# Low parts of the first stream's weight pieces by an adding DMA, and a softmax scaled negative in the masking operation

## The chip, the cores and the metric

The program runs on one core of a Trainium2 chip. The metric is the device time of one execution in microseconds (us). Before the change it is 1472.54 us, the median of 3 runs (1470.87 to 1472.68). The core has a matrix engine (PE, TensorE; its weight loads are PEld), three engines for vectors (DVE = VectorE, ACT = ScalarE, POOL = GpSimd), SP, which issues most of the DMAs, and 16 DMA engines that all queues share.

## The reference, cut to what matters

Two transformer blocks on 512 tokens of width 1024, in float32. The first block has a projection `proj = hn @ w_in`, then three kinds of attention on it, and a gated feed-forward layer; the second has a latent attention with 8 heads, a gated recurrence and a merge.

```python
def token_mixer(...):
    proj = hn @ w_in                       # q_a, k_a, v_a, q_i, k_i, w_i, q_b, k_b, v_b
    out_a = dsa_attention(...)             # 8 heads, keys chosen by a top-256 of an index score
    out_b = diff_attention(...)            # softmax(q1 k1) - lam * softmax(q2 k2), 4 heads
def first_block / second_block:
    s = where(causal, q @ k.T * scale, -inf); p = softmax(s); o = p @ v
```

The queries of every attention are normalised (rmsnorm) per head, so that the scale of a row of scores differs from token to token.

## The kernel before, in words

Products are formed from two parts of each number: `h`, the number rounded to the short format fp32r that PE multiplies at full rate, and `l`, what the rounding left. `mm3` (L217 to L220) takes three multiplications for each tile: h by h (L218), h by l (L219) and l by h (L220), all of them through PE in the order of its queue.

A weight matrix comes in pieces of 128 x 1024 numbers, 512 KB each. `split` (L167) loads a piece into a raw buffer WR (3 buffers, SP's queue), copies it to WH (4 buffers) with rounding, on ACT (L175) or POOL (L173), and subtracts: WL = WR - WH (L176, 4 buffers), on DVE or POOL. `setw` names who does it: two letters, the first for the copy ("a" ACT, "p" POOL), the second for the subtraction ("d" DVE, "p" POOL). WH and WL hold two chunks of two pieces, so the pieces of chunk c + 2 are made while PE works on chunk c + 1.

The first stream (L746 to L790) is the projection: first `w_in0` (matmuls of 452 columns), then 8 chunks of `w_inc` with 2 pieces each: keys, queries and values of two halves of the differential attention, and two chunks of queries of the chosen-key attention. Their 16 pieces are made in mode "ap". Between the multiplications of a chunk PE transposes what the chunk before has become: the outputs leave PSUM through ACT, are squared and summed per head (`head_ss`, L424; `head_scale`, L574), go through the rotation (`rope_bank`: two products on POOL, L415 and L416, two operations on DVE, L417 and L418) and come back to PE as transposes (`tr`, L437; `trr`, L441). The index score (L800 to L808) and the choice of the 256 best keys (L819, L822, on DVE) run between them. The sum over the squares of the input, `Stats.finish`, is one DVE addition (L285) before a small multiplication on PE (L287), which stands in PE's queue ahead of chunk 0.

The attentions follow, interleaved with later weight pieces of `w_xk` and `w_xv` (also "ap", L857). `soft` (L604) is their softmax: for each tile of scores a DVE operation adds the mask and takes the row's maximum (L609), a second small DVE operation multiplies it by minus the row's scale (L612), and ACT takes exp(scale * x + that) and the row's sum (L617); `recips` (L620) divides.

The order on each engine is fixed when the program is built, by a scheduler with a simulation of its own; each engine then works through its queue in order.

Of the kernel before, what the change touches and what calls it, by code (L numbers as in the profile page):

```python
# [15 lines left out]
OP = mybir.AluOpType  # L16
# [46 lines left out]
def _body(nc, tc, ctx, d):  # L63
# [57 lines left out]
    def f32(ap):  # L121
        return ap.bitcast(F32)
# [44 lines left out]
    def split(src, h, l, raw=None):  # L167
        raw = wr_()[:, :src.shape[-1]] if raw is None else raw
        nc.sync.dma_start(raw, src)
        m = wmode[wturn[0] % len(wmode)]  # L170
        wturn[0] += 1
        if m[0] == "p":
            PTS(h, raw, 1.0, 0.0, op0=OP.mult, op1=OP.add)  # L173
        else:
            ACT(h, raw, AF.Copy)  # L175
        (TT if m[1] == "d" else PTT)(l, raw, f32(h), op=OP.subtract)  # L176

    class W:

# [391 lines left out]
        c_ = slice(nt0 * P, nt0 * P + 256)  # L571
        hilo(dsts[:, 0:2, c_], dsts[:, 2:4, c_], p3)

    def head_scale(ps, nt0, out):  # L574

        s_ = head_ss(ps, 4)
        t = sm(8)
        for nn in range(2):
            TS(t[:, nn * 4:nn * 4 + 4], s_[:, nn * 4:nn * 4 + 4], st0["m64"][:, nt0 + nn:nt0 + nn + 1], None, op0=OP.add)
        if len(out.shape) == 3:  # L580
            PTT(out, t.rearrange("p (n h) -> p n h", n=2), nhalf[:, :8].rearrange("p (n h) -> p n h", n=2), op=OP.pow)
        else:
# [18 lines left out]
    s1r = kp(8)
    s1r = Ring([s1r[:, 2 * i:2 * i + 2] for i in range(4)])

    def soft(srcs, mask, scales, N, dst, su=None):  # L604

        n = len(srcs)
        mx, nb = sm(n), sm(n)
        for i in range(n):
            nc.vector.tensor_tensor_reduce(dst[i], srcs[i], mask, 1.0, LOWEST, op0=OP.add, op1=OP.max,  # L609
                                           accum_out=mx[:, i:i + 1])  # L610

            TS(nb[:, i:i + 1], mx[:, i:i + 1], scales[:, i:i + 1], -1.0, op0=OP.mult, op1=OP.mult)  # L612
        if su is None:
            su = sm(n)
            su = [su[:, i:i + 1] for i in range(n)]
        for i in range(n):
            ACT(dst[i], dst[i], AF.Exp, scale=scales[:, i:i + 1], bias=nb[:, i:i + 1], accum_out=su[i])  # L617
        return su

    def recips(su):  # L620
        ri = sm(len(su))
        for i, a in enumerate(su):
            nc.vector.reciprocal(ri[:, i:i + 1], a)
        return ri

    class Diff:
# [7 lines left out]
        def chunks(self):  # L634
            def k_mid(ps, nt0):
                rs, t = sm(8), sm(8)
                head_scale(ps, nt0, rs)
                TS(t, rs, 8.0, None, op0=OP.mult)
                return rope_bank(ps, 4, nt0, st0["tab_kb"], t)

            def q_mid(ps, nt0):
                head_scale(ps, nt0, self.qs[:, nt0 * 4:nt0 * 4 + 8])
                return rope_bank(ps, 4, nt0, st0["tab_qb"])

            def v_mid(ps, nt0):
# [15 lines left out]
        def pair(self, b, fring, rring, out):  # L661
            hf, kb, qb, vb, qs = self.hf, self.kb, self.qb, self.vb, self.qs
            N = P * (b + 1)
            om = 1.0 - LINIT
            v = {}

            def stage_a(hh):
                if hh == 0:
                    v["s1"] = s1r()
                pss = []  # L670
                for c in range(2):
                    ps = psc()[:, :N]
# [12 lines left out]
                v["a", hh] = sms[0]

            def stage_b(hh):
                a = v["a", hh]
                pt = ptr()
                for j in range(b + 1):  # L690
                    tr(pt[:, j * P:(j + 1) * P], a[:, j * P:(j + 1) * P])
                ph, pl = rring(F32R)[:, :N], rring(F32R)[:, :N]
                hilo(ph, pl, pt[:, :N])
                v["p", hh] = ph, pl

            def stage_c(hh):
                ph, pl = v["p", hh]
                if hh == 0:
                    v["po"] = out()
                po = v["po"]  # L700
                for j in range(b + 1):
                    s_ = slice(j * P, (j + 1) * P)
                    mm3(po[:, hh * P:(hh + 1) * P], ph[:, s_], pl[:, s_], vb[:, j, hh, 0], vb[:, j, hh, 1],
                        j == 0, j == b)

            def stage_d():
                po = v["po"]
# [6 lines left out]
                ACT(q1, v["s1"], AF.Square, scale=math.sqrt(EPS) / om)  # L714
# [148 lines left out]
    def dsa_unit(g, b):  # L863
# [4 lines left out]
        def stage_a():  # L868
            assert b in chosen
            v["s"] = [fD() for _ in range(4)]  # L870
            for q2 in range(2):
                pss = []
                for hh in range(2):
# [6 lines left out]
                su = soft(pss, mask, qas[:, b, g * 4 + q2 * 2:g * 4 + q2 * 2 + 2], N, dst)  # L880
                ri = recips(su)
# [363 lines left out]
    def latent_fin1(kk, nt0):  # L1245
# [83 lines left out]
    class Mla:  # L1329
# [59 lines left out]
        def unit(self, hh, b):  # L1389
# [3 lines left out]
            def stage_a():  # L1393
# [460 lines left out]
```

## Time and profile before

| | |
|---|---|
| runs, median of 3 | 1472.54 us (1470.87 to 1472.68) |
| profiled execution | 1471.03 us |
| its span, first to last instruction | 1469.2 us |
| PE busy | 1427.6 us, 97% |
| DVE busy | 972.4 us, 66% |
| ACT busy | 570.9 us, 39% |
| POOL busy | 500.8 us, 34% |
| mean granted clock of PE | 0.991 of full speed |

A clock of 1.00 is PE's upper level (2.4 GHz), 0.50 the lower (1.2 GHz); a value between them is a mean over a stretch that had both. PE's operations are pipelined, so that the time from one start to the next says more than the duration of one.

### The profile page before, as it was taken

The page shows a single profiled execution, that of the slowest core. Times are in us where ns is not written, and L with a number is a line of the kernel's source. Part 1 is how long each engine was busy: PE and PEld are TensorE (multiplying, and loading weights), DVE is VectorE, ACT ScalarE, POOL GpSimd, SP SyncE. Part 2 cuts the span into 40 slices and gives each one's busy share as a digit, 9 for nine tenths or more (in the row PEclk, how much of TensorE's full clock was granted, in tenths as well). Part 3 has the DMA queues.
Part 4 walks back from the last instruction along what each step waited for, and adds up shares of the span by engine and source line. Part 5 has one row for each costly group of instructions (what it writes and reads, how often), then busy time and mean ns, then how long its engine had stood idle before and what let it go on. Part 6 is the DMA issues. An engine that isn't in the chain of part 4 may idle for free.

```text
span 1469.2 us, 21193 instructions
## 1 busy us (share of the span) xinstructions
PE 1427.6 (97%) x7920; PEld 1237.1 (84%) x7920; DVE 972.4 (66%) x1920; ACT 570.9 (39%) x1148; POOL 500.8 (34%) x455
## 2 busy tenths in 40 slices
PE   6989999999999999999999999999999999999998
PEld 5888889888878788888888988888888898888887
DVE  8899889755445776356665556666548778885553
ACT  4535768844542322112223344444322333342121
POOL 6665666445531332223321111111114324331110
PEclk9999989999999999999999999999999999999999
DMA  6121143234213222332323432223442221257522
GB/s 215 60 72 58 44 144 117 97 97 132 90 44 101 86 89 85 99 115 89 100 76 95 129 105 94 95 95 106 139 130 86 72 100 67 93 165 239 185 65 86
DMA packets 56023, 152.69 MB, mean 104 GB/s; under 512 B 6000, under 2 KB 13680, under 8 KB 55920
## 3 DMA queue, kind: packets, MB, share of 16 engines
q1 hardware_dynamic: 55776, 151.33, 32.4%
q8 instruction: 62, 1.02, 0.3%
q14 instruction: 41, 0.34, 0.1%
q10 hardware_dynamic: 144, 0.00, 0.0%
HBM read 135.58 MB, written 15.73 MB: 103 GB/s over the span
## 4 chain that ended last, share of the span: by engine, by line
PE 81%; DVE 11%; issue 4%; ACT 2%; POOL 1%; DMA 1%; SPq 0%; POOLq 0%; DVEq 0%; ACTq 0%
PE PS L218 19%; PE PS L219 19%; PE PS L220 18%; PE PT L218 7%; PE PT L220 7%; PE PT L219 7%; PE PS L437 2%; DVE S L822 1%; DVE keep L819 1%; DVE R L155 1%; DVE WL L176 1%; PE PS L1400 1%; DVE S L808 0%; PE PS L876 0%; DMA S<-xT_d 0%
## 5 line engine op out<-in xcount | busy, mean ns | idle before, releaser
L218 PE MATMUL PS<-R,WH 128*128 128x512 f32 x920 | 358.9, 392 | 1.8 <-DVE S L1156 1.1
L219 PE MATMUL PS<-R,WH 128*128 128x512 f32 x920 | 359.6, 391 | 0.2 <-DVE R L155 0.2
L220 PE MATMUL PS<-R,WL 128*128 128x512 f32 x920 | 358.4, 391 | 0.0
L176 DVE TENSOR_TENSOR WL<-WR,WH 128x1024 fp32r<-128x1024 f32 (+4 forms) x176 | 208.5, 1187 | 110.6 <-ACT WH L175 90.6
L175 ACT ACTIVATE WH<-WR 128x1024 fp32r<-128x1024 f32 (+2 forms) x144 | 150.0, 1043 | 224.2 <-PE PS L219 150.8
L173 POOL TENSOR_SCALAR WH<-WR 128x1024 fp32r<-128x1024 f32 (+3 forms) x88 | 87.8, 997 | 356.0 <-PE PS L219 144.2
L218 PEld LDWEIGHTS PS<-R,WH 128*128 128x128 f32 x920 | 172.5, 188 | 37.6 <-DVE S L1156 1.5
L220 PEld LDWEIGHTS PS<-R,WL 128*128 128x128 f32 x920 | 173.1, 188 | 35.8
L219 PEld LDWEIGHTS PS<-R,WH 128*128 128x128 f32 x920 | 173.1, 188 | 34.7 <-DVE R L155 0.5
L218 PE MATMUL PS<-WH,R 128*128 128x256 f32 (+2 forms) x568 | 166.6, 298 | 7.4 <-POOL WH L173 5.5
L220 PE MATMUL PS<-WH,R 128*128 128x256 f32 (+2 forms) x568 | 167.6, 296 | 1.5 <-DVE R L152 1.5
L176 POOL TENSOR_TENSOR WL<-WR,WH 128x1024 fp32r<-128x1024 f32 x56 | 139.2, 2494 | 84.2 <-ACT WH L175 74.4
L219 PE MATMUL PS<-WL,R 128*128 128x256 f32 (+2 forms) x568 | 166.3, 294 | 0.9 <-DVE WL L176 0.7
L218 PE MATMUL PT<-R,WH 128*128 128x512 f32 x352 | 138.5, 394 | 0.3 <-DVE R L158 0.3
L220 PE MATMUL PT<-R,WL 128*128 128x512 f32 x352 | 137.5, 391 | 0.0
L219 PE MATMUL PT<-R,WH 128*128 128x512 f32 x352 | 137.4, 390 | 0.0
L218 PEld LDWEIGHTS PS<-WH,R 128*128 128x128 f32 x568 | 111.0, 196 | 10.6 <-POOL WH L173 5.5
L220 PEld LDWEIGHTS PS<-WH,R 128*128 128x128 f32 x568 | 110.7, 195 | 4.6 <-DVE R L152 1.9
L219 PEld LDWEIGHTS PS<-WL,R 128*128 128x128 f32 x568 | 110.5, 195 | 4.5 <-DVE WL L176 2.2
L218 PEld LDWEIGHTS PT<-R,WH 128*128 128x128 f32 x352 | 66.2, 188 | 13.9 <-DVE R L158 0.8
L220 PEld LDWEIGHTS PT<-R,WL 128*128 128x128 f32 x352 | 66.1, 188 | 13.8
L219 PEld LDWEIGHTS PT<-R,WH 128*128 128x128 f32 x352 | 66.2, 188 | 12.9
(395 smaller groups left out, 2648.7 us busy)
## 6 DMA issues: line engine op xcount, KB each, us to landing
WR<-w_fi_d SPq DMA_DIRECT2D x44, 512.0 KB, 3.7
WR<-w_inc_d SPq DMA_DIRECT2D x16, 512.0 KB, 3.7
WR<-w_fo_d SPq DMA_DIRECT2D x16, 512.0 KB, 3.7
WR<-w_gl_d SPq DMA_DIRECT2D x16, 512.0 KB, 3.3
WR<-w_xk_d SPq DMA_DIRECT2D x8, 512.0 KB, 3.7
WR<-w_xv_d SPq DMA_DIRECT2D x8, 512.0 KB, 3.7
WR<-w_out_d SPq DMA_DIRECT2D x8, 512.0 KB, 3.8
WR<-w_xq_d SPq DMA_DIRECT2D x8, 512.0 KB, 3.7
```

Source lines behind the costliest of these rows:

```text
L155: TT(ol, src, f32(oh), op=OP.subtract)
L173: PTS(h, raw, 1.0, 0.0, op0=OP.mult, op1=OP.add)
L175: ACT(h, raw, AF.Copy)
L176: (TT if m[1] == "d" else PTT)(l, raw, f32(h), op=OP.subtract)
L218: nc.tensor.matmul(ps, sh, mh, start=first, stop=False)
L219: nc.tensor.matmul(ps, sh, ml, start=False, stop=False)
L220: nc.tensor.matmul(ps, sl, mh, start=False, stop=last)
L437: nc.tensor.transpose(out, in_, ident)
L819: i = nc.vector.max(m8, sc[b])
L822: nc.vector.match_replace(sc[b], m8, sc[b], TAKEN)
L1400: nc.tensor.matmul(ps, qp[hh][:, s_], rr(kpe[j])[:, :N], start=False, stop=j == 1)
```

## The change

**The 16 pieces of w_inc.** Mode "ap" becomes "ax". In it ACT still makes WH from WR; then ACT writes WL = -WR, rounded as WH is, and POOL issues a DMA that reads the same 512 KB of the weight from memory again and adds them to WL where it lies. WL is then the weight minus its rounded value, as before. POOL no longer subtracts these pieces; ACT has 16 more copies of 128 x 1024; there are 16 more DMAs of 512 KB, on POOL's queue.

**The softmax.** The rows' scales are kept negated. The masking operation now takes such a scale as an operand and gives (x + mask) * (-scale) with the row's minimum in place of the maximum; ACT takes exp(-x + minimum). The small operation L612 is gone for all 96 tiles. For it the scales are negated by a small ACT copy (8 in the first block, one in the second).

**Small ones.** `recips` takes two columns at once, `head_scale` adds both tokens' terms in one operation with a broadcast instead of two.

```diff
-        (TT if m[1] == "d" else PTT)(l, raw, f32(h), op=OP.subtract)
+        if m[1] == "x":
+
+            ACT(l, raw, AF.Copy, scale=-1.0)
+            nc.gpsimd.dma_start(l, src, accum_op=OP.add)
+        else:
+            (TT if m[1] == "d" else PTT)(l, raw, f32(h), op=OP.subtract)
...
-        for nn in range(2):
-            TS(t[:, nn * 4:nn * 4 + 4], s_[:, nn * 4:nn * 4 + 4], st0["m64"][:, nt0 + nn:nt0 + nn + 1], None, op0=OP.add)
+        TT(t.rearrange("p (n h) -> p n h", n=2), s_.rearrange("p (n h) -> p n h", n=2),
+           bc_tok(st0["m64"], nt0, 4), op=OP.add)
...
+        r = sm(8)
+        rpow(r, t)
+        ACT(out, r.rearrange("p (n h) -> p n h", n=2), AF.Copy, scale=-1.0)
...
-            nc.vector.tensor_tensor_reduce(dst[i], srcs[i], mask, 1.0, LOWEST, op0=OP.add, op1=OP.max,
-                                           accum_out=mx[:, i:i + 1])
-
-            TS(nb[:, i:i + 1], mx[:, i:i + 1], scales[:, i:i + 1], -1.0, op0=OP.mult, op1=OP.mult)
...
-            ACT(dst[i], dst[i], AF.Exp, scale=scales[:, i:i + 1], bias=nb[:, i:i + 1], accum_out=su[i])
+            nc.vector.tensor_tensor_reduce(dst[i], src, mask, nscales[:, i:i + 1], HIGHEST, op0=OP.add, op1=OP.min,
+                                           accum_out=nb)
+            ACT(dst[i], dst[i], AF.Exp, scale=-1.0, bias=nb, accum_out=su[:, i:i + 1])
...
-    setw("ap")
+    setw("ax")
     steps(proj, "end")
```

Where it moves instructions. POOL's queue from the first piece of chunk 0 on, before the change (WL_105 and WL_106 are chunk 0, WL_107 and WL_108 chunk 1; L415 and L416 are the rotation):

```order
L176 TENSOR_TENSOR WL_105<-WR_99,WH_101 128x1024
L176 TENSOR_TENSOR WL_106<-WR_100,WH_102 128x1024
L176 TENSOR_TENSOR WL_107<-WR_98,WH_103 128x1024
L415 TENSOR_TENSOR S_82<-S_96,S_90 128x2x32
L416 TENSOR_TENSOR S_82<-S_96,S_90 128x2x32
```

The same place after the change (L421 and L422 are the rotation there):

```order
L180 DMA WL_105<-w_inc_d 128x1024
L180 DMA WL_106<-w_inc_d 128x1024
L180 DMA WL_107<-w_inc_d 128x1024
L421 TENSOR_TENSOR S_82<-S_96,S_90 128x2x32
L422 TENSOR_TENSOR S_82<-S_96,S_90 128x2x32
```

The three DMAs stand where the three subtractions stood, ahead of the rotation. ACT's queue at the same place, before:

```order
L175 ACTIVATE WH_101<-WR_99 128x1024
L175 ACTIVATE WH_102<-WR_100 128x1024
L175 ACTIVATE WH_103<-WR_98 128x1024
L490 ACTIVATE S_96<-PS_114 128x452
L490 ACTIVATE S_88<-PS_115 128x452
```

and after (L179 is the negated copy, L176 the copy to WH, L496 the move of the first results out of PSUM):

```order
L176 ACTIVATE WH_101<-WR_99 128x1024
L179 ACTIVATE WL_105<-WR_99 128x1024
L176 ACTIVATE WH_102<-WR_100 128x1024
L179 ACTIVATE WL_106<-WR_100 128x1024
L179 ACTIVATE WL_107<-WR_98 128x1024
L176 ACTIVATE WH_103<-WR_98 128x1024
L496 ACTIVATE S_96<-PS_114 128x452
```

Each negated copy stands beside its WH copy, sometimes ahead of it. DVE's queue in the attention that follows, where the first tiles of 384 columns are masked, before (L609 the masking operation, in two rows with its reading of the maximum; L623 and L683 division and factor of the pair before; L822 the choice of keys):

```order
L609 ISA S_97,SMALL<-PS_114,cst 128x512
L609 ISA SMALL 128x1
L612 TENSOR_SCALAR SMALL<-SMALL,keep 128x1
L819 MAX keep<-S_87 128x8
L623 RECIPROCAL SMALL<-SMALL 128x1
L612 TENSOR_SCALAR SMALL<-SMALL,keep 128x1
L155 TENSOR_TENSOR R_68<-PS_116,R_68 128x2x256
L822 MATCH_REPLACE S_87<-keep,S_87 128x384
L683 TENSOR_SCALAR SMALL<-keep,SMALL 128x1
L609 ISA F_73,SMALL<-PS_110,cst 128x384
```

and after (L617 is the masking operation there, with the scale as an operand in `keep`):

```order
L617 ISA S_97,SMALL<-PS_114,cst,keep 128x512
L617 ISA SMALL 128x1
L684 SCALAR_TENSOR_TENSOR S_94<-S_95,SMALL,S_94 128x512
L436 TENSOR_REDUCE SMALL<-S_85 128x8
L819 MAX keep<-S_87 128x8
L584 TENSOR_TENSOR SMALL<-SMALL,keep 128x8
L617 ISA F_73,SMALL<-PS_110,cst,keep 128x384
```

The small operations between two maskings are gone, and work of the last chunks stands in their place.

## Rows read from the trace of the kernel before

**Rows 1.** Busy time by engine in three stretches (us; instructions), clock, DMA share, GB/s
```profile
25.00:160.00 135.00, 123.51 (x934) 115.82 (x933) 127.52 (x338) 69.77 (x163) 83.86 (x68) 0.99 0.21 68
160.00:300.00 140.00, 133.47 (x961) 121.59 (x960) 114.65 (x360) 102.97 (x272) 85.69 (x75) 0.95 0.34 106
300.00:1469.20 1169.20, 1153.47 (x5965) 985.55 (x5964) 709.41 (x1171) 385.57 (x694) 317.70 (x297) 1.00 0.33 105
```
**Rows 2.** PE's waits, 25 to 172 us: us in total, times, longest
```profile
PE PS L287 <- DVE S L285: 3.5, 1, 3.5
PE PS L437 <- DVE F L418: 3.0, 2, 1.6
PE PS L437 <- ACT S L804: 1.7, 1, 1.7
PE PS L441 <- DVE Q L550: 1.7, 1, 1.7
PE PS L220 <- DVE R L155: 1.2, 1, 1.2
PE PS L437 <- DVE S L421: 0.4, 1, 0.4
```
**Rows 3.** POOL's instructions by line, 25 to 145 us: busy us, mean ns
```profile
L176 POOL TENSOR_TENSOR WL<-WR,WH 128x1024 fp32r<-128x1024 f32 x16 | 41.5, 2603 | 19.9 <-ACT WH L175 17.4 <-DVE Q L155 2.5
```
**Rows 4.** Timeline of POOL (start, duration, us): two of its subtractions' runs
```profile
25.27 8.60 POOL L176 TENSOR_TENSOR WL<-WR,WH 128x1024 fp32r<-128x1024 f32 x3 [6.54 <-ACT WH L175]
...
100.25 5.18 POOL L176 TENSOR_TENSOR WL<-WR,WH 128x1024 fp32r<-128x1024 f32 x2
```
**Rows 5.** Timeline of DVE, 25 to 35 us
```profile
25.29 0.28 DVE L395 TENSOR_TENSOR S<-S,S 128x128 f32<-128x128 f32 x1
...
29.17 2.49 DVE L395 TENSOR_TENSOR S<-S,S 128x128 f32<-128x128 f32 x1
31.59 2.42 DVE L392 TENSOR_TENSOR S<-S,S 128x128 f32<-128x128 f32 x1
...
34.26 0.80 DVE L285 TENSOR_TENSOR S<-S,S 128x512 f32<-128x512 f32 x1
```
**Rows 6.** Timeline of DVE, 94 to 106 us
```profile
94.32 0.68 DVE L418 TENSOR_TENSOR F<-F,S 128x512 f32<-128x512 f32 x1
...
100.40 2.79 DVE L418 TENSOR_TENSOR F<-F 128x512 f32<-128x512 f32 x1
103.11 2.87 DVE L417 TENSOR_TENSOR S<-S,S 128x512 f32<-128x512 f32 x1
```
**Rows 7.** Timeline of PE: first and fifth low multiplication of chunk 0, first two of chunk 4
```profile
36.34 0.41 PE L219 MATMUL PS<-WL,R 128*128 128x256 f32 x1
...
38.90 0.41 PE L219 MATMUL PS<-WL,R 128*128 128x256 f32 x1
...
98.66 0.28 PE L219 MATMUL PS<-WL,R 128*128 128x256 f32 x1
99.02 0.28 PE L219 MATMUL PS<-WL,R 128*128 128x256 f32 x1
```
**Rows 8.** Timeline of ACT: copies to WH, first piece of chunk 0 and chunk 4
```profile
24.14 1.05 ACT L175 ACTIVATE WH<-WR 128x1024 fp32r<-128x1024 f32 x1
...
84.14 1.05 ACT L175 ACTIVATE WH<-WR 128x1024 fp32r<-128x1024 f32 x1
```
**Rows 9.** DMAs by line: count, KB each, median us from issue to landing
```profile
WR<-w_inc_d SPq DMA_DIRECT2D x16, 512.0 KB, 3.7
...
R<-yb_d SPq DMA_DIRECT2D x8, 512.0 KB, 5.5
```
**Rows 10.** DVE's instructions by line, 0 to 400 us: busy us, mean ns
```profile
L612 DVE TENSOR_SCALAR SMALL<-SMALL,keep 128x1 f32<-128x1 f32 x64 | 12.7, 204 | 0.3
```
**Rows 11.** PE's longest wait, 160 to 300 us
```profile
PE PS L218 <- DVE SMALL L609: 4.1, 4, 2.3
```

More of the change, by code (lines that the diff above doesn't have):

```diff
@@ L29 @@
 LOWEST = -3.0e38
+HIGHEST = 3.0e38
 TAKEN = -3.4e38
@@ L572, in pair_fin, with head_scale @@
         hilo(dsts[:, 0:2, c_], dsts[:, 2:4, c_], p3)
-    def head_scale(ps, nt0, out):
+    def head_scale(ps, nt0, out, neg=False):
         s_ = head_ss(ps, 4)
         t = sm(8)
-        for nn in range(2):
-            TS(t[:, nn * 4:nn * 4 + 4], s_[:, nn * 4:nn * 4 + 4], st0["m64"][:, nt0 + nn:nt0 + nn + 1], None, op0=OP.add)
-        if len(out.shape) == 3:
-            PTT(out, t.rearrange("p (n h) -> p n h", n=2), nhalf[:, :8].rearrange("p (n h) -> p n h", n=2), op=OP.pow)
-        else:
+        TT(t.rearrange("p (n h) -> p n h", n=2), s_.rearrange("p (n h) -> p n h", n=2),
+           bc_tok(st0["m64"], nt0, 4), op=OP.add)
+        if not neg:
             rpow(out, t)
+            return
+        r = sm(8)
+        rpow(r, t)
+        ACT(out, r.rearrange("p (n h) -> p n h", n=2), AF.Copy, scale=-1.0)
     qi = rr(R[7]).rearrange("p (h c) -> p h c", h=4)
@@ L600, in _body, with soft @@
     Ob = Halves([R[5], R[10]])
[L601 to L608, printed above, removed]
-            nc.vector.tensor_tensor_reduce(dst[i], srcs[i], mask, 1.0, LOWEST, op0=OP.add, op1=OP.max,
-                                           accum_out=mx[:, i:i + 1])
-            TS(nb[:, i:i + 1], mx[:, i:i + 1], scales[:, i:i + 1], -1.0, op0=OP.mult, op1=OP.mult)
[L613 to L616, printed above, removed]
-            ACT(dst[i], dst[i], AF.Exp, scale=scales[:, i:i + 1], bias=nb[:, i:i + 1], accum_out=su[i])
-        return su
+    s1r = kp(16)
+    s1r = Ring([s1r[:, 4 * i:4 * i + 4].rearrange("p (h c) -> p h c", h=2) for i in range(4)])
+    def soft(srcs, mask, nscales, N, dst, su):
+        for i, src in enumerate(srcs):
+            nb = sm(1)
+            nc.vector.tensor_tensor_reduce(dst[i], src, mask, nscales[:, i:i + 1], HIGHEST, op0=OP.add, op1=OP.min,
+                                           accum_out=nb)
+            ACT(dst[i], dst[i], AF.Exp, scale=-1.0, bias=nb, accum_out=su[:, i:i + 1])
     def recips(su):
-        ri = sm(len(su))
-        for i, a in enumerate(su):
-            nc.vector.reciprocal(ri[:, i:i + 1], a)
+        ri = sm(su.shape[-1])
+        nc.vector.reciprocal(ri, su)
         return ri
@@ L641, in q_mid @@
             def q_mid(ps, nt0):
-                head_scale(ps, nt0, self.qs[:, nt0 * 4:nt0 * 4 + 8])
+                head_scale(ps, nt0, self.qs[:, nt0 * 4:nt0 * 4 + 8].rearrange("p (n h) -> p n h", n=2), True)
                 return rope_bank(ps, 4, nt0, st0["tab_qb"])
@@ L678, in stage_a @@
                 sms = [fring()[:, :N] for _ in range(2)]
-                s1 = v["s1"][:, hh:hh + 1]
-                su = soft(pss, cmask(b), qs[:, b * 4 + hh * 2:b * 4 + hh * 2 + 2], N, sms, [s1, sm(1)])
+                s12 = v["s1"][:, hh]
+                soft(pss, cmask(b), qs[:, b * 4 + hh * 2:b * 4 + hh * 2 + 2], N, sms, s12)
                 c2 = sm(1)
-                TS(c2, s1, recips(su[1:]), nlam, op0=OP.mult, op1=OP.mult)
+                TS(c2, recips(s12[:, 1:2]), s12[:, 0:1], nlam, op0=OP.mult, op1=OP.mult)
                 STT(sms[0], sms[1], c2, sms[0], op0=OP.mult, op1=OP.add)
@@ L713, in stage_d @@
                         accum_out=ssq[:, hh:hh + 1])
-                ACT(q1, v["s1"], AF.Square, scale=math.sqrt(EPS) / om)
+                ACT(q1, v["s1"][:, :, 0], AF.Square, scale=math.sqrt(EPS) / om)
                 for hh in range(2):
@@ L741, in mid @@
         def mid(ps, nt0):
-            head_scale(ps, nt0, qas[:, nt0:nt0 + 2, g * 4:g * 4 + 4])
+            head_scale(ps, nt0, qas[:, nt0:nt0 + 2, g * 4:g * 4 + 4], True)
             return stack_mid(ps, nt0, st0["tab_qa"])
@@ L870, in stage_a @@
             v["s"] = [fD() for _ in range(4)]
+            su = sm(4)
             for q2 in range(2):
@@ L879, in stage_a @@
                 dst = [v["s"][q2 * 2 + hh][:, :N] for hh in range(2)]
-                su = soft(pss, mask, qas[:, b, g * 4 + q2 * 2:g * 4 + q2 * 2 + 2], N, dst)
-                ri = recips(su)
+                s2 = su[:, q2 * 2:q2 * 2 + 2]
+                soft(pss, mask, qas[:, b, g * 4 + q2 * 2:g * 4 + q2 * 2 + 2], N, dst, s2)
+                ri = recips(s2)
                 for hh in range(2):
@@ L1258, in latent_fin1 @@
         STT(t, t, 0.5, m192, op0=OP.mult, op1=OP.add)
-        rpow(qsc, t)
+        rpow(t, t)
+        ACT(qsc, t, AF.Copy, scale=-1.0)
         for k in range(3):
@@ L1401, in stage_a @@
                 e = sM()[:, :N]
-                su = soft([ps], cmask(b), qsc[:, b:b + 1], N, [e])
-                PTS(e, e, recips(su)[:, 0:1], 0.0, op0=OP.mult, op1=OP.add)
+                su = sm(1)
+                soft([ps], cmask(b), qsc[:, b:b + 1], N, [e], su)
+                PTS(e, e, recips(su), 0.0, op0=OP.mult, op1=OP.add)
                 v["e"] = e
```

## The prediction

> **What bounds the kernel now.** I read the busy times by stretch first. From 300 us to the end PE is busy 1153.47 of 1169.20 us, 98.7% [rows 1]; nothing that the change does to other engines can give much there. The room lies ahead of it: from 25 to 160 us PE is idle for 135.00 - 123.51 = 11.5 us, and from 160 to 300 us for 140.00 - 133.47 = 6.5 us, where its clock also averages 0.95 [rows 1]. In the first of these stretches DVE is busy 127.52 of 135 us, so it is close to being a second bound [rows 1].
>
> The list of PE's waits says who ends the idle time: 3.5 us before L287 (the small multiplication ahead of chunk 0), and 3.0 + 1.7 + 1.7 + 1.2 + 0.4 = 8.0 us before transposes and one multiplication whose operands come late from DVE or ACT [rows 2]. Together that is 11.5 us, all of the idle time. No wait there names a weight piece: the pieces are ready in time.
>
> Then the timeline says why DVE is late. While POOL runs its three subtractions from 25.27 to 33.87 us [rows 4], DVE takes 2.49 and 2.42 us for operations on 128x128 that took 0.28 us just before [rows 5]. It looks the same at 100.25 to 105.43 us: two subtractions on POOL [rows 4], and DVE's L418 and L417 on 128x512 last 2.79 and 2.87 us, where L418 took 0.68 us at 94.32 [rows 6]. So a DVE operation on two operands that meets a POOL subtraction is held for about the length of that subtraction (mean 2.60 us, 16 of them, 41.5 us [rows 3]). That is an interference of the two engines as the rows show it, and the change takes those 16 subtractions away.
>
> **The change part by part.**
>
> *Start of chunk 0.* L285, for which PE waits 3.5 us, starts at 34.26 us behind the two held operations [rows 5]. Without the hold these save 2.49 + 2.42 - 2 x 0.28 = 4.3 us, so L285, done at 34.26 + 0.80 = 35.1 us now, would be done by 30.8 us, before PE begins to wait for it at 35.1 - 3.5 = 31.6 us [rows 2, 5]. The 3.5 us would go. What is late next is WL. The first copy to WH ends at 24.14 + 1.05 = 25.2 us [rows 8]; the negated copy, of the same shape, ends at 26.2 us; then the adding DMA has to land. The trace has no adding DMA. A plain load of 512 KB lands 3.7 us after its issue, the slowest group of that size 5.5 us [rows 9]. The adding one also has to read its destination, so I take twice the plain one, 7.4 us, as an estimate from that row; it lands at 33.6 us. PE first multiplies by it at 36.34 us now [rows 7] and would want it 3.5 us earlier, at 32.8 us, so 0.8 us of waiting comes back: gain 2.7 us. The lower end of the DMA is 3.7 us (gain 3.5), the upper one unknown. With the gap goes its follower: after it PE needs 2.56 us for four triples (36.34 to 38.90, 0.64 each) and later 0.36 for one (98.66 to 99.02) [rows 7], which is 1.1 us for these four; I count half of it, 0.5, as a short wait remains. First term: **-3.2 us**.
>
> A page prices such a DMA: the Trainium skill, "DMA: Bandwidth & Descriptors", section on the anatomy of one DMA, fits about 2.0 us plus bytes over 436 GB/s for DMAs from POOL's queue. Taken so, an estimate for 512 KB is 3.2 us, the 0.8 us of waiting would be nought, and the term about 1.4 us larger; the plain loads here, at 3.7 us [rows 9], are a little slower than that fit.
>
> *The other waits to 172 us.* They sum to 8.0 us [rows 2], and the two cases shown lose some 2 us in each hold. Released by about 2 us per hold (16 holds at most, 32 us of DVE's 127.52), DVE no longer fills the stretch, and waits of 1.2 to 1.7 us each should close. I count all 8.0. Against it stands ACT: 16 more copies of 1.05 us [rows 8], 17 us on an engine busy 69.77 of 135 us [rows 1]. It rises to some 64%, and a copy that stands ahead of an operation on the way to a transpose delays it by up to 1.05 us. Bounds: 0, and 8 chunks times 2 copies, 17 us, if none was covered; most are covered by PE's own work on the chunk, so I take 1.5 us. Second term: **-6.5 us**.
>
> *Whether the pieces come in time later.* PE first uses a low piece of chunk 4, one of those with the least room, at 98.66 us [rows 7], and the copy of its first piece ends at 85.2 us [rows 8]: 13.5 us, less 1.05 for the negated copy, leaves about 12.4 us for POOL's queue and the DMA. At 7.4 us this costs nothing. POOL's queue holds rotations behind each DMA, as it did behind each subtraction; the DMA's issue waits for ACT alone, the subtraction waited for ACT too and then worked 2.60 us, so the rotations start earlier or the same. What POOL spends on issuing is not in the trace: between nothing and the 2.60 us of a subtraction; I take 1 us, nearer to a plain issue, and it hides either way.
>
> *Softmax and small ones.* 64 of the 96 small operations lie before 400 us and take 12.7 us of DVE [rows 10]; the other 32 lie in the latent attention, where PE is saturated, and count nothing. The masking operation gets an operand more: between nothing and the 0.204 us of the operation it replaces. 12 small additions and 16 reciprocals fewer save some 0.2 us each on DVE, by that same row; 9 small ACT copies are added, all long before their use. From 160 to 300 us PE waits 4.1 us for L609 to free a score bank [rows 11], with DVE 82% busy, not full; the reordered queue can also make such a wait longer. Bounds: a gain of 6.5 idle us plus some 2 for the clock, a loss of 3 like the longest single wait with a little on top. I take **-1.5 us**.
>
> Sum: 3.2 + 6.5 + 1.5 = 11.2 us. The profiled execution took 1471.03 us, 1.8 more than its span; minus 11.2 it is 1459.8 us. The median of the three runs is 1.5 us above that execution, so on that scale: **1461 us**.
>
> **The rivals.**
>
> *More goes.* The attentions profit as well: the 6.5 idle us and the low clock there vanish along with the whole of the first two terms. 3.5 + 1.1 + 8.0 + 6.5 = 19.1 us, so 1453.5 us. For it: its waits are on DVE, which loses 13 us of work there. Against: 20 subtractions on POOL for later weights remain and go on holding DVE, and DVE is not full there.
>
> *Half of it.* The waits pass from DVE to ACT or to POOL's small operations, which stand in the same chains; only the start of chunk 0 and some 2 us are won: 5 us, 1467.5 us. For it: one of the five waits names ACT [rows 2].
>
> *The hold stays.* Writing the descriptors of the adding DMA on POOL might hold DVE as the subtraction did, so the change would do on POOL what it was to take off. Then 0, with ACT's work on top 0 to 1 us: 1472.5 us. For it: whatever POOL does with a second operand held DVE. Against: a DMA issue reads no tile of 512 KB through POOL.
>
> *Slower: the adding DMA lands late.* Place: the first L219 of each chunk. Price: with a landing time L a piece with as little room as that of chunk 4 waits L - 12.4 us; I count four of the eight chunks as such. It decides from about L = 15 us, where four times 2.6 us eat the 11 us; at 20 us, four times 7.6 less 11 is +19, 1492 us. For it: the operation is new here, and DVE keeps two-operand work going nearly without pause. Against: 15 us is four times the plain load.
>
> The Trainium skill, "DMA: Bandwidth & Descriptors", section on SWDGE, HWDGE and iDMA, speaks for this rival: POOL writes its descriptors into rings in SBUF, and DVE can lock POOL out of SBUF in its two-port modes. No run here shows such a ring; what the rows show is POOL's subtractions keeping a mean of 2.60 us [rows 3] beside a DVE that is 94% busy, so POOL's accesses do not wait long.
>
> **How the numbers follow.** What a measurement of this kernel can tell from no change is about 0.2%, 2.9 us. Forecast 0.46 (1456 to 1466 on its own), more goes 0.17, half of it 0.16, the hold stays 0.10, slower 0.11. All of the first two and most of the third (0.13) are faster: 0.76. The rest of the third and most of the fourth are within 0.2%: 0.12. Slower: 0.12. The range leaves out the slower rival and the lowest part of the first one: 1451 to 1472 us.
>
> **What would show it.** In the profile after: no operation of DVE on 128x128 over 1 us between 25 and 35 us; PE's wait for L285 gone, and the first L219 of chunk 0 near 33.6 us instead of 36.34; a clock of 1.00 from 35 to 40 us; PE idle from 25 to 160 us down from 11.5 to about 3 us; DVE's busy time in that stretch some 30 us lower; adding DMAs that land within 12 us. I am wrong if PE waits for WL at several chunks (the DMA is late), if DVE's long operations stay (the hold is POOL's DMA work as well), or if the idle time is the same with ACT named in place of DVE.

## The result and the profile after

The changed kernel takes 1460.41 us, the median of 4 runs (1458.28 to 1461.97), beside 1472.61 us (4 runs, 1470.87 to 1473.16) for the kernel before on the same chip: a ratio of 0.9921, 95% interval 0.9905 to 0.9936. Its profiled execution took 1458.28 us with a span of 1456.5 us, 12.7 us less than the span before.

Lines have moved by the change: the three multiplications are now L224 to L226 (L225 the low one), the addition of the input's squares is L291, the negated copy L179, the adding DMA L180, the subtraction L182, the rotation L421 to L424, and the softmax's masking operation L617.

Busy time by engine in the same three stretches, columns as in [rows 1] (PE, PEld, DVE, ACT, POOL, then clock, DMA share, GB/s):

```profile
25.00:160.00 135.00, 131.03 (x1010) 124.45 (x1009) 109.08 (x332) 90.50 (x205) 63.59 (x74) 0.97 0.56 134
160.00:300.00 140.00, 133.54 (x937) 121.46 (x936) 101.09 (x281) 98.13 (x264) 82.03 (x71) 0.95 0.37 114
300.00:1456.50 1156.50, 1139.79 (x5906) 974.09 (x5904) 700.20 (x1132) 376.81 (x686) 313.18 (x296) 1.00 0.33 105
```

PE's idle time from 25 to 160 us is 4.0 us in place of 11.5. DVE's busy time there went from 127.52 to 109.08 us, ACT's from 69.77 to 90.50. The second stretch has the same 6.5 idle us and the same clock of 0.95 as before. PE's waits from 25 to 172 us, the answer to [rows 2]:

```profile
PE PS L225 <- DMA WL<-w_inc_d: 4.0, 1, 4.0
PE PS L224 <- DVE SMALL L617: 1.4, 2, 0.9
```

All six waits of [rows 2] are gone. There is one new one, for the first adding DMA; the 1.4 us for L617 lie behind 160 us, in the attentions, which this kernel reaches some 10 us earlier. DVE's timeline at the place of [rows 5]:

```profile
25.15 0.29 DVE L400 SCALAR_TENSOR_TENSOR S<-S,S 128x128 f32<-128x128 f32 x1
...
26.43 0.75 DVE L153 SCALAR_TENSOR_TENSOR R<-S,vec,R 128x512 fp32r<-128x512 f32 x1
27.09 0.28 DVE L401 TENSOR_TENSOR S<-S,S 128x128 f32<-128x128 f32 x1
27.30 0.29 DVE L398 TENSOR_TENSOR S<-S,S 128x128 f32<-128x128 f32 x1
...
27.70 0.69 DVE L291 TENSOR_TENSOR S<-S,S 128x512 f32<-128x512 f32 x1
```

None of these operations is long any more, and the addition of the squares ends at 28.4 us in place of 35.1. POOL's timeline says what it does meanwhile (start, duration, in brackets the idle time before and what ended it):

```profile
26.51 1.06 POOL L180 DMA_DIRECT2D WL<-w_inc_d  x1 [7.05 <-DVE S L400]
28.41 0.86 POOL L180 DMA_DIRECT2D WL<-w_inc_d  x1 [0.83 <-DVE S L291]
```

The brackets name DVE, but what the two issues follow is ACT: both start 0.3 us after the end of their negated copies (26.20 and 28.10 us in ACT's timeline). The first issue lasts from 26.51 to 27.57 us; the three two-operand operations of DVE that begin in that time take 0.28 to 0.29 us. Of the 28 that begin during any of the 16 issues, none is more than 0.3 us longer than the shortest of its kind and shape. So the issue does not hold DVE as a subtraction did. PE's timeline, then the DMAs by line (count, KB, median us from issue to landing), then two stretches of 5 us in the columns above:

```profile
34.97 0.58 PE L225 MATMUL PS<-WL,R 128*128 128x256 f32 x1 [3.97 <-DMA WL<-w_inc_d]
```
```profile
WR<-w_inc_d SPq DMA_DIRECT2D x16, 512.0 KB, 7.6
WL<-w_inc_d POOLq DMA_DIRECT2D x16, 512.0 KB, 9.0
```
```profile
30.00:35.00 5.00, 1.03 (x9) 0.82 (x9) 2.52 (x10) 3.38 (x7) 3.34 (x7) 0.74 1.01 233
35.00:40.00 5.00, 5.00 (x26) 5.00 (x27) 2.92 (x11) 4.97 (x13) 4.41 (x8) 0.58 1.05 271
```

PE waits from 31.0 to 34.97 us, 8.5 us after the DMA's issue began, and then runs at a mean clock of 0.58: between the two levels, nearer to the lower. The DMA engines are full in both stretches (share 1.01 and 1.05), and the plain loads of the same weights land after 7.6 us in place of 3.7 [rows 9].

### The profile page after: what moved, and what is told of

Its sections match the earlier page's. It is cut to its first block, busy times and chain, and to the rows that moved or that the text cites. A ratio compares the mean times of both kernels' runs of the same rounds, so it can differ in the third digit from the quotient of the medians.

```text
span 1456.5 us, 21098 instructions
## 1 busy us (share of the span) xinstructions
PE 1422.8 (98%) x7920; PEld 1235.8 (85%) x7920; DVE 931.1 (64%) x1796; ACT 578.0 (40%) x1173; POOL 473.2 (32%) x455
## 4 chain that ended last, share of the span: by engine, by line
PE 70%; DVE 4%; issue 3%; POOL 2%; ACT 1%; DMA 0%; POOLq 0%; DVEq 0%; ACTq 0%
PE PS L225 16%; PE PS L224 16%; PE PS L226 16%; PE PT L224 6%; PE PT L226 6%; PE PT L225 6%; PE PS L443 1%; DVE WL L182 1%; PE PS L1403 1%; DVE R L156 1%; DMA gate_d<-S 0%; POOL F L1578 0%; ACT R L155 0%; DVE S L1527 0%; DVE Q L156 0%
## 5 line engine op out<-in xcount | busy, mean ns | idle before, releaser
L224 PE MATMUL PS<-R,WH 128*128 128x512 f32 x920 | 359.2, 393 | 1.8 <-DVE S L1158 1.0
L225 PE MATMUL PS<-R,WH 128*128 128x512 f32 x920 | 359.7, 391 | 0.2 <-DVE R L156 0.2
L226 PE MATMUL PS<-R,WL 128*128 128x512 f32 x920 | 358.6, 391 | 0.0
L182 DVE TENSOR_TENSOR WL<-WR,WH 128x1024 fp32r<-128x1024 f32 (+4 forms) x176 | 206.3, 1174 | 113.7 <-ACT WH L176 92.6
L176 ACT ACTIVATE WH<-WR 128x1024 fp32r<-128x1024 f32 (+2 forms) x144 | 150.1, 1042 | 218.9 <-PE PS L225 153.9
L224 PEld LDWEIGHTS PS<-R,WH 128*128 128x128 f32 x920 | 172.5, 188 | 37.5 <-DVE S L1158 1.5
L226 PEld LDWEIGHTS PS<-R,WL 128*128 128x128 f32 x920 | 172.9, 188 | 35.4
L225 PEld LDWEIGHTS PS<-R,WH 128*128 128x128 f32 x920 | 172.9, 188 | 34.7 <-DVE R L156 0.5
L224 PE MATMUL PS<-WH,R 128*128 128x256 f32 (+2 forms) x568 | 166.5, 299 | 7.4 <-POOL WH L174 5.5
L225 PE MATMUL PS<-WL,R 128*128 128x256 f32 (+2 forms) x568 | 167.3, 296 | 4.1 <-DMA WL<-w_inc_d 4.0
L226 PE MATMUL PS<-WH,R 128*128 128x256 f32 (+2 forms) x568 | 166.7, 295 | 1.0 <-DVE R L153 1.0
L224 PE MATMUL PT<-R,WH 128*128 128x512 f32 x352 | 138.7, 394 | 0.3 <-DVE R L159 0.3
L225 PE MATMUL PT<-R,WH 128*128 128x512 f32 x352 | 137.7, 391 | 0.0
L226 PE MATMUL PT<-R,WL 128*128 128x512 f32 x352 | 137.7, 391 | 0.0
L224 PEld LDWEIGHTS PS<-WH,R 128*128 128x128 f32 x568 | 111.2, 196 | 10.4 <-POOL WH L174 5.5
L182 POOL TENSOR_TENSOR WL<-WR,WH 128x1024 fp32r<-128x1024 f32 x40 | 97.5, 2447 | 64.3 <-ACT WH L176 59.4
L225 PEld LDWEIGHTS PS<-WL,R 128*128 128x128 f32 x568 | 110.8, 195 | 7.8 <-DMA WL<-w_inc_d 4.2
L226 PEld LDWEIGHTS PS<-WH,R 128*128 128x128 f32 x568 | 110.8, 195 | 3.2 <-DVE R L153 1.4
L147 POOL TENSOR_TENSOR SMALL<-SMALL,nhalf 128x2 f32<-128x2 f32 (+3 forms) x43 | 48.6, 1141 | 97.7 <-DVE SMALL L1770 42.6
L224 PEld LDWEIGHTS PT<-R,WH 128*128 128x128 f32 x352 | 66.2, 188 | 13.9 <-DVE R L159 0.8
L226 PEld LDWEIGHTS PT<-R,WL 128*128 128x128 f32 x352 | 66.1, 188 | 13.6
```

What stands on the lines that cost most here:

```text
L147: PTT(out, x, nhalf[:, :n], op=OP.pow)
L224: nc.tensor.matmul(ps, sh, mh, start=first, stop=False)
L225: nc.tensor.matmul(ps, sh, ml, start=False, stop=False)
L226: nc.tensor.matmul(ps, sl, mh, start=False, stop=last)
```

## The experiments

To see where time goes, one place in the program is followed through all profiles: when PE starts a given low multiplication (first of chunk 0, 1, 4 and 7; the 33rd on the weights that come after), and the span. Differences to before, us, one profiled execution each; the ratio is from the timed runs, each against runs of before on the same chip.

| kernel | chunk 0 | 1 | 4 | 7 | later | span | ratio, 95% interval |
|---|---|---|---|---|---|---|---|
| before, at | 36.34 | 51.90 | 98.66 | 158.11 | 203.02 | 1469.2 | 1 |
| whole change | -1.4 | -2.8 | -7.4 | -9.7 | -9.6 | -12.7 | 0.9921 (0.9905 to 0.9936) |
| e1 DMA alone | -0.9 | -2.1 | -6.7 | -10.5 | -7.9 | -7.5 | 0.9940 (0.9926 to 0.9953) |
| e2 softmax alone | +0.6 | -0.2 | -0.6 | +1.8 | +1.3 | -1.4 | 0.9999 (0.9990 to 1.0008) |
| e3 no adding DMA | -4.8 | -6.7 | -10.8 | -13.9 | -13.1 | -11.8 | 0.9907 (0.9893 to 0.9921) |
| e4 two on DVE | -5.0 | -2.1 | -6.3 | -9.0 | -9.4 | -9.2 | 0.9926 (0.9913 to 0.9939) |
| e5 all 16 on DVE | -5.1 | -7.7 | -12.3 | -16.1 | -13.8 | -9.4 | 0.9932 (0.9920 to 0.9944) |
| e6 later ones too | -1.4 | -2.9 | -7.4 | -9.8 | -6.8 | +7.0 | 1.0048 (1.0033 to 1.0063) |
| e7 one operand | -2.8 | -1.3 | -1.0 | -0.1 | -0.4 | -1.3 | 0.9995 (0.9987 to 1.0004) |
| e8 plain DMA | -2.3 | -4.2 | -8.8 | -11.1 | -11.0 | -14.7 | 0.9904 (0.9891 to 0.9917) |
| f1 four later on DVE | +0.2 | -1.6 | -6.2 | -8.5 | -10.6 | -10.0 | 0.9916 (0.9903 to 0.9930) |
| f2 all later on DVE | -1.1 | -3.0 | -7.5 | -9.9 | -11.8 | -3.4 | 0.9957 (0.9944 to 0.9969) |
| f3 16 + 4 on DVE | -4.7 | -7.3 | -11.9 | -15.7 | -16.9 | -15.6 | 0.9884 (0.9870 to 0.9897) |
| f4 first + 4 on DVE | -5.2 | -3.8 | -6.3 | -10.7 | -14.8 | -12.3 | 0.9918 (0.9904 to 0.9931) |

Theory 1: the gain is that POOL's subtractions no longer hold DVE. Theory 2: it is the work that the softmax takes off DVE.

**e1, the DMA alone** (into the kernel before, with the change's branch for "x" in `split`, which is not shown again):

```diff
-    setw("ap")
+    setw("ax")
```


> Only the first part of the change: the 16 low parts by a negated copy on ACT and an adding DMA; softmax as before. Theory 1 (the gain is that POOL's subtractions no longer hold DVE): 1462 to 1464 us, ratio 0.993 to 0.995, PE idle from 25 to 160 us near 4 us as with the whole change. Theory 2 (the gain is that the softmax takes some 13 us of work off DVE): 1468 to 1472 us.

1463.01 us, with PE idle for 4.5 us from 25 to 160 us. Theory 1 as expected, theory 2 not.

**e2, the softmax and the small ones alone** (in the changed kernel):

```diff
-    setw("ax")
+    setw("ap")
```


> Only the second part: the softmax scaled negative, with the 16 subtractions on POOL as before. Theory 1: 1469 to 1472 us, and the first low multiplication of chunk 0 near 36.3 us as before. Theory 2: 1461 to 1465 us. If the parts add, its gain and that of the DMA alone sum to the 12 us of both.

1471.09 us, no difference to before, and PE is idle for 11.3 us from 25 to 160 us (11.5 before). DVE's timeline shows the hold as in [rows 5]:

```profile
28.93 2.48 DVE L401 TENSOR_TENSOR S<-S,S 128x128 f32<-128x128 f32 x1
31.34 2.42 DVE L398 TENSOR_TENSOR S<-S,S 128x128 f32<-128x128 f32 x1
```

The softmax alone is worth nothing that can be measured. Beside the DMA it may be worth something: the whole change is 2.6 us below e1 by the medians, but the two intervals overlap.

**e7, POOL's work put back, on one operand** (in the changed kernel):

```diff
-            ACT(l, raw, AF.Copy, scale=-1.0)
-            nc.gpsimd.dma_start(l, src, accum_op=OP.add)
+            for _ in range(3):
+                PTS(l, raw, 1.0, 0.0, op0=OP.mult, op1=OP.add)
```


> The changed kernel with each of the 16 low parts replaced by three POOL operations on one operand of the same size (the subtraction itself is left out of the computation), so that POOL is busy at least as long as with the subtractions. Theory 1a (only a POOL operation that reads two operands holds DVE): no DVE operation on 128x128 over 1 us beside them, time 1459 to 1463 us. Theory 1b (any POOL operation holds DVE): operations of over 2 us as before, 1468 to 1474 us.

1469.81 us: the gain is gone. POOL's timeline, then DVE's:

```profile
26.53 2.12 POOL L180 TENSOR_SCALAR WL<-WR 128x1024 fp32r<-128x1024 f32 x2 [2.83 <-PE PS L226]
```
```profile
26.65 1.06 DVE L778 TENSOR_TENSOR F<-S 128x64 f32<-128x64 f32 x1
27.64 1.15 DVE L400 SCALAR_TENSOR_TENSOR S<-S,S 128x128 f32<-128x128 f32 x1
28.71 0.28 DVE L401 TENSOR_TENSOR S<-S,S 128x128 f32<-128x128 f32 x1
```

Two POOL operations of 1.06 us each lie there; each holds one DVE operation (L400 takes 0.29 us in the changed kernel, above) for about its own length, and when they are done DVE is quick again. Theory 1b holds but for its size: one operand on POOL is enough, and a hold is as long as the POOL operation, here 1 us and not 2.4. Not all of the loss in e7 is holds, though. POOL is busier in it than before (98.55 against 83.86 us from 25 to 160 us), and of the 8 us that PE idles there 2.5 us are a wait for POOL itself, which is late with WL.

The holds can be counted: of DVE's operations from 25 to 145 us, the table takes every one that lasts over 0.6 us more than the shortest of the same kind and shape in the whole trace, and adds what is above that shortest.

| kernel | such operations | above the shortest, us | longest |
|---|---|---|---|
| e2 softmax alone | 13 | 26.1 | 2.2 |
| before | 15 | 25.8 | 2.2 |
| e7 one operand | 16 | 13.5 | 0.9 |
| e1 DMA alone | 2 | 2.7 | 2.1 |
| e5 all on DVE | 1 | 2.0 | 2.0 |
| whole change | 1 | 1.2 | 1.2 |

The kernels with many holds take 1470 to 1473 us, those without 1460 to 1463. Of the 15 before, 13 lie beside a subtraction and two beside POOL's small rotation operations; the one that is left in the whole change, at 80.69 us, lies beside rotations too, so these also hold DVE, for less time. The longest in e1 (79.73 us, 2.1 us over) begins during an issue of the DMA and has two rotations beside it; what share each has in it was not told apart.

One rival has to be set aside. Whatever takes the subtractions off POOL also frees POOL's queue, in which the rotations stand behind them, and that alone might be the gain. The trace of the kernel before speaks against it: no wait of PE in [rows 2] names POOL, POOL is idle for 51 of the 135 us, and from 25 to 160 us DVE waits for it once:

```profile
DVE F L418 <- POOL S L416: 0.5, 1, 0.5
```

Of PE's 11.5 us, 6.6 stand right behind a held operation of DVE in the trace before: the 3.5 us for L285; the 1.7 us for L550, which follows a held L761 (2.26 us); and 1.4 us for L418, itself held (2.79 us [rows 6]). For the other 4.9 us, which come later in the same queue, the link to the holds is argued from their going with them.

**e5, all 16 subtracted by DVE itself** (in the changed kernel):

```diff
-    setw("ax")
+    setw("ad")
```


> The changed kernel with all 16 low parts subtracted on DVE (about 1.2 us each, as its two subtractions took in the run before this one) in place of the adding DMA: no POOL subtraction holds DVE before 145 us, no extra copies on ACT, no extra transfers, but 16 x 1.2 = 19.5 us more work on DVE. Theory 1 (each POOL subtraction costs DVE about 2 us, more than doing it itself): 1463 to 1467 us. Rival (DVE is the second bound, so that its busy time counts and not the hold): 1470 to 1476 us, since DVE is as full as before.

1460.85 us, below theory 1's own figure and level with the adding DMA. Busy times, then PE's longest waits from 25 to 172 us (all three behind 160 us):

```profile
25.00:160.00 135.00, 133.87 (x1041) 126.46 (x1039) 125.89 (x348) 78.16 (x192) 57.98 (x57) 1.00 0.22 71
```
```profile
PE PS L447 <- ACT R L566: 1.7, 1, 1.7
PE PS L224 <- DVE SMALL L617: 1.5, 2, 0.9
PE PS L224 <- ACT WH L176: 1.4, 1, 1.4
```

DVE is as busy as before (125.89 against 127.52 us), yet PE is idle for 1.1 us in place of 11.5. DVE's share of the time said little: before, part of it was waiting. Up to chunk 7 this kernel is 6 us ahead of the changed one, and it gives that back in the attentions (-16.1 to -9.4).

**e3, the adding DMAs left out, and e8, plain ones in their place** (in the changed kernel):

```diff
-            nc.gpsimd.dma_start(l, src, accum_op=OP.add)     # e3: without this line
+            nc.gpsimd.dma_start(l, src)                      # e8: this one in its place
```


> The changed kernel without the adding DMAs (WL holds the negated high part, so the low parts' term is left out of the computation); the negated copies stay. It shows what is left of the DMA's price. Theory 1: only the wait for WL of 4.0 us and the low clock behind it (some 1.6 us) go: about 1455 us. Rival A (the wait hides other waits): 1459 to 1461 us. Rival B (the 8 MB of extra transfers and POOL's issues slow other work too): under 1452 us.

> The changed kernel with the 16 DMAs of POOL's queue plain in place of adding (WL then holds the weight itself, the subtraction is left out of the computation). It asks why the adding DMA lands 9.0 us after its issue and the loads beside it 7.6 in place of 3.7. If the adding is what costs: landing 4 to 5 us, loads near 4, and PE's wait for WL of 4.0 us under 1 us. If POOL's queue or the two transfers side by side cost: landing 7 to 9 us, loads 6 to 8, and the time as that of the changed kernel, 1459 to 1461 us.

e3: 1458.50 us, between theory 1's 1455 and rival A; PE runs from 25 to 160 us almost without a gap, at a clock of 1.00:

```profile
25.00:160.00 135.00, 134.03 (x1043) 126.74 (x1042) 113.21 (x340) 92.83 (x213) 49.60 (x58) 1.00 0.24 73
```

At chunk 7 it is 4.2 us ahead of the changed kernel, in the timed runs 2 us, with overlapping intervals. e8: 1456.59 us. Its DMAs by line:

```profile
WR<-w_inc_d SPq DMA_DIRECT2D x16, 512.0 KB, 5.2
WL<-w_inc_d POOLq DMA_DIRECT2D x16, 512.0 KB, 5.0
```

Adding makes the landing 9.0 us and not 5.0, and the loads beside it 7.6 and not 5.2; without the second transfer they take 3.8 (e3). So the first hypothesis is nearer for the landing, and the two transfers side by side cost the loads 1.4 us more. PE's wait for WL fell only to 2.5 us, not under 1: in the crowded start, with the DMA engines full, the first plain DMA lands some 7.5 us after its issue (26.53 to 34.0 us).

**e4, the two pieces of chunk 0 on DVE** (in the changed kernel):

```diff
-    setw("ax")
+    setw("ad", "ad", *["ax"] * 14)
```


> The changed kernel with the first two of the 16 pieces (those of chunk 0) subtracted on DVE, the other 14 by the adding DMA. Theory 1: the wait for WL at 35 us goes, the clock stays at 1.00 from 35 to 40 us: 1455 to 1457 us. Rival: two subtractions of 1 us or more on DVE delay its chain to chunk 0, so the wait only changes its name: 1459 to 1462 us.

1460.67 us, the rival's time, but not for the rival's reason: chunk 0 starts 5.0 us earlier, and 3 of them are lost by chunk 1. ACT's timeline, then PE's:

```profile
40.17 1.06 ACT L176 ACTIVATE WH<-WR 128x1024 fp32r<-128x1024 f32 x1 [3.28 <-DMA WR<-w_inc_d]
41.13 1.04 ACT L179 ACTIVATE WL<-WR 128x1024 fp32r<-128x1024 f32 x1
42.08 1.05 ACT L530 ACTIVATE R<-S,keep 128x64 fp32r<-128x64 f32 x4
43.03 1.05 ACT L530 ACTIVATE R<-F,keep 128x64 fp32r<-128x64 f32 x4
43.99 0.40 ACT L525 ACTIVATE Q<-F 128x256 fp32r<-128x256 f32 x1
```
```profile
44.44 0.28 PE L447 MATMUL PS<-identr,Q 128*128 128x128 f32 x1 [2.69 <-ACT Q L525]
```

ACT waits 3.28 us for a raw piece that has not landed, and behind its copies in the queue stands L525, for which PE then waits 2.69 us. What SP's queue waited for from 20 to 45 us, the two longest:

```profile
SPq L170 <- DMA WR<-w_inc_d: 11.3, 2, 7.3
SPq L170 <- DVE WL L182: 7.5, 2, 4.8
```

A load waits here for DVE to have read the raw buffer, and for a transfer; which of the two made this piece late was not told apart.

**e6, the adding DMA for the next 40 pieces too** (in the changed kernel, at L857):

```diff
-    setw("ap")
+    setw("ax")
```


> The changed kernel with the adding DMA also for the next 40 pieces (145 to 427 us), which POOL still subtracts in it. In its trace the longest wait of the attentions (3.83 us at 175 us) stands behind a DVE operation of 2.81 us that lies beside such a subtraction. Theory 1: that wait and others from 160 to 300 us go, 1453 to 1457 us. Rival (40 more copies on ACT and 40 more transfers that slow the loads come late for a PE that is nearly always busy): 1460 to 1470 us.

1477.68 us. Theory 1's forecast fell here, and the rival's was still too low. PE's waits from 160 to 450 us that name a low part, the DMAs by line, and the busy times:

```profile
PE PS L225 <- DMA WL<-w_xk_d: 7.0, 2, 4.3
PE PS L226 <- DMA WL<-w_xq_d: 4.3, 1, 4.3
PE PS L226 <- DMA WL<-w_out_d: 2.8, 3, 1.4
```
```profile
WR<-w_xk_d SPq DMA_DIRECT2D x8, 512.0 KB, 8.5
WL<-w_xk_d POOLq DMA_DIRECT2D x8, 512.0 KB, 9.2
```
```profile
300.00:450.00 150.00, 140.31 (x677) 116.08 (x676) 53.12 (x102) 83.42 (x138) 40.97 (x49) 0.98 0.66 151
```

The DMA takes about the same time (7.8 to 9.2 us by weight), but these pieces have less time to land: 14.1 us of waits for low parts, where the changed kernel has none. From 300 to 450 us PE is idle for 9.7 us (1.6 in the changed kernel).

**f1, f2, f3, f4: the next pieces on DVE.** In the changed kernel the longest wait from 160 to 300 us again lies beside a POOL subtraction. POOL's, DVE's and PE's timelines of the changed kernel:

```profile
171.77 2.35 POOL L182 TENSOR_TENSOR WL<-WR,WH 128x1024 fp32r<-128x1024 f32 x1
```
```profile
171.85 2.81 DVE L424 TENSOR_TENSOR S<-S,S 128x512 f32<-128x512 f32 x1
174.59 0.74 DVE L617 CUSTOM_DVE_ANT_0 S<-PS,cst,keep 128x512 f32<-128x512 f32 x1
```
```profile
175.39 0.79 PE L224 MATMUL PS<-R,R 64*128 64x512 f32 x1 [3.83 <-DVE SMALL L617]
```

```diff
-    setw("ap")                                      # L857, the next 40 pieces
+    setw(*["ad"] * 4, *["ap"] * 36)                 # f1, f3, f4
+    setw("ad")                                      # f2
-    setw("ax")                                      # L767, the first 16
+    setw("ad")                                      # f3
+    setw("ad", *["ax"] * 15)                        # f4
```


> The changed kernel with the first 4 of the next 40 pieces (at 146 to 182 us) subtracted on DVE, the other 36 on POOL as before. Theory 1 (the 3.83 us wait at 175 us comes from DVE being held by POOL's subtraction at 171.8 us): that wait goes but for the 1.2 us of DVE's own subtraction, 1455 to 1458 us. Rival (the start of the attentions waits for its own chain of softmax and rotation, whatever POOL does): another wait takes its place, 1459 to 1462 us.

> The changed kernel with all 40 next pieces (145 to 427 us) subtracted on DVE: 40 x 1.2 = 49 us more work for it, in place of 40 x 2.4 = 96 us in which POOL may hold it. Theory 1: 1454 to 1458 us. Rival (in the attentions DVE is 95% busy from 200 to 220 us, so its own 1.2 us count in full there): 1461 to 1467 us.

> All 16 first pieces and the first 4 of the next 40 on DVE, no adding DMA. The version with the 16 on DVE was 16.6 us ahead of before at 150 us and gave 5 of it back in the attentions. If POOL's subtractions at 158 to 179 us are why: 1454 to 1457 us. If the start of the attentions is bound by its own chain: 1459 to 1462 us.

> The first of the 16 pieces on DVE, the other 15 by the adding DMA, and the first 4 of the next 40 on DVE. Both waits that are left in the changed kernel are aimed at: that for WL at 35 us (4.0 us with its low clock) and that at 175 us (3.83 us). Theory 1: both go, 1452 to 1456 us. Rival (each is given back by the next wait of the chain, as with two pieces on DVE): 1458 to 1461 us.

f1: 1459.91 us, the rival. The wait of 3.83 us is gone; PE still waits 2.1 us for L617 and 1.4 us for a copy to WH there, and in this execution chunk 0 began 1.6 us later than in the changed kernel. f2: 1466.87 us, the rival's time, but not shown to be for the rival's reason. Until PE's 1700th operation (at 259.9 us before) it is 13.4 us ahead of before, the changed kernel 12.3. By the 1900th (290.9 us) it is 8.1 ahead against 12.5: from 255 to 260 us its clock is at 0.50, with PE busy throughout. Another 3.0 us go at 400 us, where PE waits for ACT (L155). f4: 1459.72 us, the rival: its second piece, still an adding DMA, now makes PE wait 3.0 us in chunk 0. f3: 1455.35 us, theory 1: it beats the changed kernel (the intervals of the two ratios, 0.9870 to 0.9897 and 0.9905 to 0.9936, do not meet) and has no adding DMA at all. The start of the attentions in the changed kernel, then in f3:

```profile
160.00:170.00 10.00, 8.55 (x58) 6.98 (x57) 7.67 (x20) 9.44 (x22) 6.73 (x5) 0.95 0.34 93
170.00:180.00 10.00, 6.17 (x27) 4.70 (x27) 6.98 (x15) 5.22 (x15) 7.35 (x7) 0.50 0.36 119
```
```profile
160.00:170.00 10.00, 5.23 (x32) 4.14 (x31) 7.33 (x16) 6.83 (x19) 8.94 (x7) 0.74 0.58 169
170.00:180.00 10.00, 9.78 (x68) 8.74 (x68) 9.17 (x20) 6.53 (x16) 6.58 (x5) 0.91 0.45 145
```

PE idles for 5.3 us in the one and 5.0 in the other. In f3 nearly all of it lies in the first ten us, and in the second the clock is back at 0.91; in the changed kernel the long wait ends at 175.39 us, and the clock is at the lower level for all of the second ten us.

## Why the prediction was right, and where its sizes were off

**The cause.** DVE held by POOL's subtractions: shown by taking them away in two ways (DMA, e1; DVE, e5) and by leaving them (e2); e7, with other POOL work in their place, agrees, but part of its loss is POOL's own lateness. The 26 us of holds counted are below the 32 that the prediction allowed at most. The Trainium skill, "SBUF — State Buffer", section "Who interferes with whom", states the rule: a DVE instruction with two SBUF inputs contends with a POOL instruction that reads SBUF, and the one that starts second waits for the whole of the other. The rows agree: an operation of DVE on 128x128 takes 2.4 us beside a subtraction, 1.15 us beside a one-operand operation, and 0.28 us beside a DMA issue.

**First term, the start of chunk 0: forecast -3.2 us, measured -1.4.** The wait for L291 went, and L291 ended even earlier than worked out (28.4 us, forecast 30.8): before, a third operation had been held that the prediction left out.

```profile
26.36 2.88 DVE L152 SCALAR_TENSOR_TENSOR R<-S,vec,R 128x512 fp32r<-128x512 f32 x1
```

It takes 0.75 us in the changed kernel (L153, above). What was mis-sized in this term is the landing time: forecast 7.4 us after an issue at 26.2, measured 8.5 after 26.51, which is 1.4 us. The rest is the clock: the forecast counted half of its 1.1 us as saved, and 35 to 40 us ran at 0.58. In the kernel before the same stretch had 0.66, so nothing was saved there:

```profile
35.00:40.00 5.00, 4.88 (x28) 4.88 (x29) 4.50 (x23) 1.79 (x4) 1.68 (x3) 0.66 0.34 98
```

The smaller estimate that the prediction set beside its sum, 3.2 us, was further off: even the plain DMA from POOL's queue took 5.0 us (e8; the shortest 3.8).

**Second term, the other waits to 172 us: forecast -6.5, measured -8.3** (-9.7 at chunk 7 less -1.4; without the softmax, in e1, about -9.5). All 8.0 us of [rows 2] closed; the 1.5 us for ACT's copies did not show, though ACT's busy time rose by 20.7 us.

**Pieces in time later.** As forecast: 9.0 us are within the 12.4 us of room, and no chunk but the first waits. POOL's issue takes 0.86 to 1.18 us, estimated at 1.

**Third term, softmax and attentions: forecast -1.5, measured -3.0** (-9.7 to -12.7), in single executions of a kernel whose four runs differ by up to 3.7 us. Of it 2.4 us come between the 33rd and the 65th low multiplication on the later weights (203 to 223 us before), where e1, without the softmax, gains 0.4; so part of it lies in the attentions, as forecast. PE's idle time from 160 to 300 us did not shrink from 6.5 us, so "more goes" fell, and the wait for L609 that the term was worked out from is not shown to be what it saved.

**The sum** was 11.2 us, measured 12.7 in the profiled executions and 12.2 by the medians: the first term too large by 1.8, the others too small by 3.3. That it came out within 1.5 us is in part luck, as these errors cancel.

**The other rivals.** "The hold stays" fell, since the operations that begin during an issue of the changed kernel are quick, and "half of it" fell, since from 25 to 160 us no wait of PE passed to ACT or to POOL's operations. The slower rival did not come about here, since the DMA lands within its room; in e6 it did, at the same landing time and less room.

**Signs that failed.** DVE's busy time from 25 to 160 us fell by 18 us and not by 30, since the changed kernel is up to 10 us further on in that window. Up to the same multiplication, the first low one of chunk 7, it is 125.96 us before and 99.54 after, 26 us less, which is near the forecast. The clock was 0.58 from 35 to 40 us and not 1.00.

**Open.** What the softmax is worth beside the DMA (2.6 us by medians, intervals overlap). And why the attentions give back part of the lead in some kernels (e1, e3, e5) and not in others: the 16 pieces on DVE give back 6.7 us of 16.1 alone (e5), the 4 later ones win nothing alone (f1), and together they give back next to nothing (f3); this was measured and not explained. Nor is it explained why the clock of f2 falls near 254 us.

## What to carry to other kernels

Before work is moved from DVE to POOL to balance them, look at DVE's own operations beside it. Here one that took nine times its usual time (2.49 against 0.28 us) was being held, and the work was cheaper on DVE (1.2 us a piece) than beside it (2.4 us on POOL and up to 2.2 us of DVE's time). That held for the first 16 pieces and the 4 behind them (e5, f3); all 40 of the later ones on DVE made the kernel slower than the changed one (f2), so it has to be tried place by place. An engine's busy share does not tell working from being held; the shortest duration of the same operation does. An adding DMA can replace a subtraction only where its landing time, 9 us here, fits between the last write of its destination and the first use.

## What the runs showed that was not expected

- An adding DMA of 512 KB from POOL's queue lands after 9.0 us (median; 7.2 to 12.1 in the changed kernel), a plain one from the same queue after 5.0 (3.8 to 9.0), and while adding ones run, plain loads of the same size take 7.6 in place of 3.7 us.
- POOL's issue of the adding DMA takes 0.91 us, of the plain one 0.61 (medians of 16).
- The hold works the other way too. In e7, beside a DVE that works without a gap, two of POOL's one-operand operations take 4.71 us in place of 2.1, and the first alone 3.70:

```profile
31.37 4.71 POOL L180 TENSOR_SCALAR WL<-WR 128x1024 fp32r<-128x1024 f32 x2 [2.71 <-DMA WR<-w_inc_d]
```
